# Moving most stores to DRAM from SyncE's queue to GpSimd's queue

## The chip, the cores and the metric

The kernel runs on one core of one Trainium2 chip. The core has five engines with an instruction stream each: TensorE (PE, with its weight loads as PEld), VectorE (DVE), ScalarE (ACT), GpSimd (POOL) and SyncE (SP). An engine works through its stream in order. A transfer between DRAM and on-chip memory (a DMA) is issued by an instruction of one of these streams, and is then carried out by the core's 16 DMA engines. An issue that needs data waits in its stream until the data are there, and what stands behind it in that stream waits too. The metric is the device time of one execution, in microseconds (us).

## The reference, cut to what matters

One layer of a decoder step in fp32, for 1024 tokens of a prompt and 8 samples of 4 tokens (1056 columns in all). Two branches read the same normed input, their results are merged by gates, and a gated ConvFFN follows:

```python
h = rmsnorm(x, norm_mix_g)
z = h @ w_in                                   # 1024 -> 6432 columns
u = zc[..., :D_CONV] * sigmoid(zc[..., D_CONV:])
c, new_conv = causal_dwconv(conv_buf, u, conv_dw_w, conv_dw_b)   # 31 taps
ya = silu(layernorm(c, conv_ln_g, conv_ln_b)) @ w_conv_out
...
# RWKV-7, per token and head of 64:
S = S * w_t + (S a_t) b_t^T + v_t k_t^T ;  y = S r_t
...
yb = ((groupnorm(y) + bonus) * gout) @ w_rw_out
m = gates[..., :D] * ya + gates[..., D:] * yb
x = x + m @ w_mix_out
up = rmsnorm(x, norm_ffn_g) @ w_up             # 1024 -> 6144
f = gelu(conv3(up)[..., :D_FF]) * conv3(up)[..., D_FF:]
x = x + f @ w_down
y = rmsnorm(x, norm_final_g)
```

It also returns the new states: the last 30 convolution inputs, the last projected row, the matrix state S, and the last two up-projected rows.

## The kernel before

**Matmuls.** An fp32 product is split in three products of a faster format: each weight tile (128 x 1024) is loaded raw (L47, `wraw<-w_in`), copied by ScalarE to a high part (L48, `whi`), and VectorE takes the rest as a low part (L49, `wlo`). All matmuls pass through one helper (L54), so rows are told apart by tile: `mm` is a projection of 128 x 352 columns (a block is a third of the 1056 columns), the others (`w`, `c`, `y`) are the small products of the recurrence. There is one buffer for the raw tile before the tail, and two for each part.

**Stages.** `build` runs these after each other.
- Load and norm of the input (0 to some 27 us).
- `mixer_a`: projections of the convolution branch (L324, its 31 taps on VectorE at L359), of the low-rank factors (L553), of the first r, k and v tiles (L457), and the low-rank outputs (L583). Intermediate results that don't fit on chip are stored to DRAM and read back later (`d_cv`, `d_k`, `d_r`, `d_v`, `d_cum`, `d_alr`, `d_gout`).
- `mixer_b` (some 300 to 1380 us): the recurrence. 16 chains, n = 0 to 15, one for each pair of a group of four heads (J) and a quarter of the prompt (q). For each n there is a prep (L892), a stage (L999), a combine (L1065), the chain itself (L1093, it needs the state that chain n-1 left, but for q = 0, where it starts from zeros that GpSimd writes at L1113 and L1115) and a group norm (L1163). The samples' recurrence goes beside it. The remaining projections (r, k, v, gates, convolution output) are the fillers: `drive` (L708) puts them between the steps of the recurrence, by a clock that counts TensorE columns.
- The tail (some 1380 us to the end): merge, output projection and the ConvFFN.

**The turn.** A stage builds triangular 32 x 32 blocks LQ on TensorE and VectorE, stores them (`dL<-LQ`, L1026), loads them back broadcast over the lanes (`L<-dL`, L1028, 512 KB), solves them in 31 steps of two instructions on VectorE (L1034 and L1036, tiles `tm` and `X`), stores the result (`dX<-X`, L1038), and loads it back into LQ (`LQ<-dX`, L1042). Only then can the combine of this n begin. GpSimd clears one block of LQ in each quarter of a stage (L1015) and a tile P in each prep (L910).

**Queues.** In the kernel before, SyncE issues every transfer but eight: loads of weights, stores of intermediate results, the turns, and the outputs. The eight are loads of small parameters at the start, which GpSimd issues (L168). The order of each engine's stream is settled when the program is built: the framework's scheduler takes the instructions by its own estimate of when each can run. A transfer also takes one of eight completion lanes of its kind (SyncE's kind or GpSimd's kind), and waits for the transfer that had this lane before it.

Of the kernel before, what the change touches and what calls it, by code (L numbers as in the profile page):

```python
# [31 lines left out]
class Net:  # L32
# [317 lines left out]
    def conv_taps(self, cv, i):  # L350
        nc = self.nc
        cp, hs, us = cv
        while i not in us:
            yield 1
        c, u, v = us[i]
        cc = slice(i * 128, (i + 1) * 128)
        nc.scalar.activation(out=c[:, 0:TP], in_=u[:, 0:TP], func=AF.Identity, scale=self.col("conv_w", i), bias=self.col("conv_b", i))
        for t in range(1, CW):
            nc.vector.scalar_tensor_tensor(out=c[:, 0:TP], in0=u[:, t:t + TP], scalar=self.col("conv_w", t * 4 + i), in1=c[:, 0:TP],  # L359
                                           op0=ALU.mult, op1=ALU.add)  # L360
            yield

        pr = self.T4("cpr")[:, 0:8 * 4 * CW].rearrange("p (b t w) -> p b t w", b=8, w=CW)
        wt = self.par["conv_w"].rearrange("p (o w i) -> p o w i", o=1, i=4)[:, :, :, i].to_broadcast([128, 8, CW])
        for t in range(4):
            nc.gpsimd.tensor_tensor(out=pr[:, :, t], in0=v[:, :, t:t + CW], in1=wt, op=ALU.mult)
        nc.vector.tensor_reduce(out=c[:, TP:T].rearrange("p (b t) -> p b t", t=4), in_=pr, axis=AX.X, op=ALU.add)
        nc.scalar.activation(out=c[:, TP:T], in_=c[:, TP:T], func=AF.Identity, bias=self.col("conv_b", i))
        nc.sync.dma_start(out=self.d_cv[:, i], in_=c[:, :T])

        ps = self.pw_tile()
        nc.tensor.transpose(ps[:30, 0:128], u[:, TP:TP + 30], self.ident)
        for hf in range(2):
            b = cp.tile([128, 120], F32, tag="cc", name="cc")
            nc.gpsimd.tensor_copy(out=b.rearrange("p (b t) -> p b t", t=30), in_=v[:, hf * 4:hf * 4 + 4, 4:34])
            nc.tensor.transpose(ps[:120, 128 * hf + 128:128 * hf + 256], b, self.ident)
        st = cp.tile([120, 384], F32, tag="cst", name="cst")
        nc.scalar.activation(out=st[:30, 0:128], in_=ps[:30, 0:128], func=AF.Copy)
        nc.scalar.activation(out=st[:, 128:384], in_=ps[:120, 128:384], func=AF.Copy)
        nc.sync.dma_start(out=self.o["p_conv"][0, 0][:, cc], in_=st[:30, 0:128])  # L380
        so = self.o["s_conv"][0].rearrange("b i c -> (b i) c")
        for hf in range(2):
            nc.sync.dma_start(out=so[hf * 120:(hf + 1) * 120, cc], in_=st[:, 128 * hf + 128:128 * hf + 256])

    NLN, LNW = 8, 132

    def ln_block(self, b):

        nc = self.nc
        W = self.LNW  # L390
        s = slice(b * W, (b + 1) * W)
        up = lambda t: t.rearrange("p (o t) -> p o t", o=1).to_broadcast([128, 4, W])
        C, Q = self.T2([128, 4, W], "lnC"), self.T2([128, 4, W], "lnQ")

        def fold(t):

            nc.vector.tensor_tensor(out=Q[:, 0:2], in0=t[:, 0:2], in1=t[:, 2:4], op=ALU.add)
            nc.vector.tensor_tensor(out=Q[:, 0], in0=Q[:, 0], in1=Q[:, 1], op=ALU.add)
        nc.sync.dma_start(out=C, in_=self.d_cv[:, :, s])
        fold(C)  # L400
        yield self.W_LN
        ps = self.pw_tile()
        self.mm(ps[:, 0:W], self.o512, Q[:, 0], True, True)
        nc.vector.tensor_tensor(out=C, in0=C, in1=up(ps[:, 0:W]), op=ALU.subtract)
        nc.scalar.activation(out=Q, in_=C, func=AF.Square)
        fold(Q)
        yield self.W_LN
        ps = self.pw_tile()
        self.mm(ps[:, 256:256 + W], self.o512, Q[:, 0], True, True)
        rs = self.rsqrt((Q[:, 0], Q[:, 1], Q[:, 2]), ps[:, 256:256 + W], 1.0, 1e-5)  # L410
        nc.vector.tensor_tensor(out=C, in0=C, in1=up(rs), op=ALU.mult)
        for i in range(4):
            nc.scalar.activation(out=C[:, i], in_=C[:, i], func=AF.Identity, scale=self.col("cln_g", i), bias=self.col("cln_b", i))
        nc.scalar.activation(out=Q, in_=C, func=AF.Tanh, scale=0.5)
        nc.vector.scalar_tensor_tensor(out=C, in0=Q, scalar=1.0, in1=C, op0=ALU.add, op1=ALU.mult)
        nc.sync.dma_start(out=self.d_cs[:, :, s], in_=C)

    def conv_in(self):

# [12 lines left out]
    def conv_out(self, i):  # L432

        nc, a = self.nc, self.a
        job = lambda i: self.wjob(a["w_conv_out"][0][:, i * 128:(i + 1) * 128], 4)
        w = job(0) if i == 0 else self.cw
        ga = self.cvp.tile([128, T], F32, tag="ga", name="ga", bufs=2)
        nc.sync.dma_start(out=ga, in_=self.d_ga[i])
        if i < ND - 1:
            self.cw = job(i + 1)  # L440
        yield from self.project_g(w, self.cs, 4, lambda b, s, ps: nc.vector.scalar_tensor_tensor(
            out=ga[:, s], in0=ga[:, s], scalar=1.0, in1=ps, op0=ALU.add, op1=ALU.mult))
        nc.sync.dma_start(out=self.d_ma[i], in_=ga)

    def gate(self, i, x):

# [10 lines left out]
    def rkv_tile(self, j, n):  # L457

        nc = self.nc
        jj = (8, 0, 16)[n] + j  # L460
        t = self.T4("krv"[n])
        c0 = ZR + jj * 128
        yield from self.shifted(self.wjob(self.a["w_in"][0][:, c0:c0 + 128]), jj, t)
        nc.sync.dma_start(out=self.d_rkv[n][j // 2][:, j % 2], in_=t)
        self.done.add(("rkv", j, n))

    def shift_state(self):
# [115 lines left out]
    def lora_out(self, j):  # L583
# [27 lines left out]
        cum = self.T4("lc")[:, :T]  # L611
        nc.vector.tensor_tensor_scan(out=cum, data0=rst, data1=sg, initial=0.0, op0=ALU.mult, op1=ALU.add)
        for t, dst in ((cum, self.d_cum), (al, self.d_alr), (go, self.d_gout)):
            nc.sync.dma_start(out=dst[j // 2][:, j % 2], in_=t)


    def wkv_consts(self):
# [216 lines left out]
    def s_shift(self):  # L834

        nc = self.nc
        yield from self.wait(*[("rkv", j, x) for j in range(ND) for x in range(3)])
        for g in range(7):
            yield from self.take(1)
            ps = self.pw_tile()  # L840
            n = 0
            for j in range(4 * g, min(4 * g + 4, NSH)):
                w = min(128, 3360 - j * 128)
                self.tr(ps[:9, n:n + w], self.shcol[:w, j], self.ident[:w, :w])
                n += w
            st = self.T2([9, 512], "sh")
            nc.scalar.activation(out=st[:, :n], in_=ps[:9, :n], func=AF.Copy)
            nc.sync.dma_start(out=self.o["p_shift"][0][:, g * 512:g * 512 + n], in_=st[0:1, :n])
            nc.sync.dma_start(out=self.o["s_shift"][0][:, g * 512:g * 512 + n], in_=st[1:9, :n])
            self.t2_left += 1  # L850
            yield 5000

# [39 lines left out]
    def prep(self, n):  # L892
# [79 lines left out]
        for u in ([slice(0, 1), slice(1, 2)] if smp else [slice(0, 2)]):  # L972
# [1 line left out]
            pv = ps[:, :(u.stop - u.start) * W].rearrange("p (u t) -> p u t", t=W)  # L974
            self.mm(pv, self.bones, t1[:, u], True, True)
            nc.vector.tensor_tensor(out=bv[:, u], in0=pv, in1=v[:, u], op=ALU.mult)
        nc.sync.dma_start(out=self.d_bv[J][:, :, 256 * q:256 * q + 256], in_=bv[:, :, 0:256])

        if smp:
            nc.gpsimd.tensor_copy(out=self.sbv[:, 2 * J % 4:2 * J % 4 + 2], in_=bv[:, :, 256:288])  # L980
# [182 lines left out]
    def group_norm(self, n):  # L1163
# [3 lines left out]
        if q == 3:  # L1167
            yield 800
            ps = self.pw_tile()
            for u in range(2):  # L1170
                self.tr(ps[:64, 128 * u:128 * u + 128], Sf[:, 64 * u:64 * u + 64], self.ident)
            so = self.T2([64, 256], "so")
            nc.scalar.activation(out=so, in_=ps[:64, :256], func=AF.Copy)
            nc.sync.dma_start(out=self.o["p_wkv"][0, 0, 4 * J:4 * J + 4].rearrange("h v k -> v h k"),
                              in_=so.rearrange("p (h k) -> p h k", h=4))
        s = slice(256 * q, 256 * q + 256)
        ld = []
# [22 lines left out]
            self.y_split(slice(2 * J, 2 * J + 2), s, y1)  # L1200
            self.done.add(("y", n))
        else:
            nc.sync.dma_start(out=self.d_y[J][:, :, s], in_=y1)

    def free(self):

# [22 lines left out]
    def samples_in(self, j):  # L1229
# [16 lines left out]
        Sb = self.T2([128, 8, 64], "Sb")  # L1246
        AX_ = self.T2([128, 8, 64], "AXs")
        nc.scalar.activation(out=Sb, in_=ps.rearrange("p (b t) -> p b t", t=64), func=AF.Copy)
        nc.sync.dma_start(out=self.d_S[j], in_=Sb.rearrange("p b t -> p (b t)"))
        ar = ARs.rearrange("p (o q) t -> p o q t", o=1).to_broadcast([128, 8, 2, 32])  # L1250
        mb = self.mb.rearrange("p b (o t) -> p b o t", o=1).to_broadcast([128, 8, 2, 32])
        nc.vector.tensor_tensor(out=AX_.rearrange("p b (q t) -> p b q t", q=2), in0=ar, in1=mb, op=ALU.mult)
# [13 lines left out]
        nc.scalar.activation(out=UV[96:128], in_=ps[0:32, 64:128], func=AF.Copy)  # L1266
        sB = self.T2([64, 128], "sB")
        nc.scalar.activation(out=sB, in_=ps[0:64, 128:256], func=AF.Copy)
        nc.sync.dma_start(out=self.d_BT[j], in_=sB)
        yield 2000  # L1270

        G = self.pw_tile()
# [8 lines left out]
    def samples_steps(self, j0):  # L1281
# [32 lines left out]
        nc.vector.tensor_tensor(out=y1, in0=y1, in1=go, op=ALU.mult)  # L1314
        for n in range(4):
            j = j0 + n
            nc.sync.dma_start(out=self.d_y[j // 2][:, j % 2, TP:T], in_=y1[:, n])

    def samples_state(self, j):

# [17 lines left out]
        for g in range(2):  # L1338
# [4 lines left out]
                self.tr(ps[:64, b * 128:(b + 1) * 128], Sn[:, 4 * g + b], self.ident)  # L1343
            nc.scalar.activation(out=so, in_=ps[:64].rearrange("p (b t) -> p b t", t=128), func=AF.Copy)
            for x in range(2):
                nc.sync.dma_start(out=self.o["s_wkv"][0, 4 * g:4 * g + 4, 2 * j + x].rearrange("b v k -> v b k"),
                                  in_=so[:, :, 64 * x:64 * x + 64])


# [142 lines left out]
    def ffn_up(self, g, fp, cp, uH, uL, rs):  # L1492
# [10 lines left out]
        for n in range(G):  # L1503
            i = g * G + n
            cu = []
            for x in range(2):
# [24 lines left out]
                def rows(n=n, x=x, lr=lr):  # L1531
# [2 lines left out]
                    nc.scalar.activation(out=so[x][:, n * 128:(n + 1) * 128], in_=ps[:18, 0:128], func=AF.Copy)  # L1534
                    if n == G - 1:
                        c = slice(x * DF + g * G * 128, x * DF + (g + 1) * G * 128)
                        nc.sync.dma_start(out=of[0][:, c], in_=so[x][0:16])
                        nc.sync.dma_start(out=of[1][:, c], in_=so[x][16:18])
                self.late.append(rows)

                c = cp.tile([128, T], F32, tag=f"c{x}", name="c", bufs=1)
# [144 lines left out]
```

## Time and profile before

| | before |
|---|---|
| median of the runs | 2556.56 us (2561.31, 2556.56, 2546.82) |
| the profiled execution's own time | 2551.31 us |
| its span, first to last instruction | 2549.6 us |
| mean granted TensorE clock | 0.911 of 2.4 GHz |
| TensorE busy | 2372.1 us, 93% |
| VectorE busy | 1645.4 us, 65% |
| ScalarE busy | 866.1 us, 34% |
| GpSimd busy | 91.9 us, 4% |
| bytes moved by DMA | 230.61 MB, mean 90 GB/s |

The profile is of one execution on the chip. Busy time leaves out the instructions that only issue a transfer or wait for a semaphore, so SyncE has no busy time, and what it issues and waits for is seen in the views of its queue (SPq). TensorE has two clock levels, 1.2 and 2.4 GHz; a granted clock of 0.75 in a stretch is the mean over time at the one and at the other.

### The profile page before, as it was taken

What the parts mean: (1) busy time and instruction counts of PE and PEld (TensorE: products, weight loads), DVE (VectorE), ACT (ScalarE), POOL (GpSimd) and SP (SyncE); (2) the same over time, 40 slices, a digit from 0 to 9 for tenths busy, and PEclk for the clock granted to TensorE, in tenths of its full rate; (3) what the DMA queues carried; (4) which work ended last, traced back from release to release, by engine and by line L of the source; (5) the groups of instructions that cost most, each with busy time, mean ns of one, the idle gap of its engine ahead of it and who ended that gap; (6) DMA issues with size and microseconds to landing.
All of it is one profiled execution on the core that took longest, in us unless ns stands there. A gap on an engine that the chain in (4) does not pass through costs nothing.

```text
span 2549.6 us, 41402 instructions
## 1 busy us (share of the span) xinstructions
PE 2372.1 (93%) x16094; PEld 2147.3 (84%) x16094; DVE 1645.4 (65%) x4174; ACT 866.1 (34%) x1716; POOL 91.9 (4%) x248
## 2 busy tenths in 40 slices
PE   6789989977798789898999999999999999999998
PEld 5778977766676577677778999999999999999998
DVE  5999766777767876786674344465554555545556
ACT  4234332433344344333344222333221322213225
POOL 2301100000000000000000000000000000000000
PEclk9999987966676788689999999999999999999999
DMA  4124443323232343434344664431111111111111
GB/s 123 48 82 161 157 115 83 89 69 100 77 98 63 81 115 85 104 92 117 85 114 137 215 188 137 127 128 44 44 47 48 43 51 44 47 47 40 54 51 69
DMA packets 307637, 230.61 MB, mean 90 GB/s; under 512 B 90492, under 2 KB 287123, under 8 KB 306921
## 3 DMA queue, kind: packets, MB, share of 16 engines
q1 hardware_dynamic: 307185, 227.80, 30.7%
q8 instruction: 127, 2.08, 0.3%
q14 instruction: 69, 0.57, 0.1%
q0 software_dynamic: 256, 0.17, 0.0%
HBM read 157.45 MB, written 70.45 MB: 89 GB/s over the span
## 4 chain that ended last, share of the span: by engine, by line
PE 58%; DVE 4%; DMA 3%; ACT 1%; issue 0%; SPq 0%; DVEq 0%; ACTq 0%
PE mm L54 50%; PE w L54 3%; DMA L<-dL 2%; PE c L54 1%; PE y L54 1%; PE w L61 1%; DMA hL<-d_y 1%; DVE tm L1034 0%; DVE X L1036 0%; PE w L1427 0%; PE w L1512 0%; DMA dX<-X 0%; DVE E L1018 0%; PE mm L1648 0%; PE w L1533 0%
## 5 line engine op out<-in xcount | busy, mean ns | idle before, releaser
L54 PE MATMUL mm<-hH,whi 128*128 128x352 f32 (+1 forms) x2568 | 878.1, 342 | 10.4 <-DVE bcol L496 9.1
L54 PE MATMUL mm<-hH,wlo 128*128 128x352 f32 (+1 forms) x2568 | 855.7, 335 | 20.6 <-DVE wlo L49 20.6
L54 PE MATMUL mm<-hL,whi 128*128 128x352 f32 (+1 forms) x2568 | 857.0, 334 | 0.2 <-DVE hL L248 0.2
L54 PEld LDWEIGHTS mm<-hH,whi 128*128 128x128 f32 (+1 forms) x2568 | 494.5, 193 | 38.3 <-DVE bcol L496 11.2
L54 PEld LDWEIGHTS mm<-hH,wlo 128*128 128x128 f32 (+1 forms) x2568 | 494.9, 193 | 33.0 <-DVE wlo L49 23.1
L54 PEld LDWEIGHTS mm<-hL,whi 128*128 128x128 f32 (+1 forms) x2568 | 495.9, 193 | 10.0 <-issue 1.2
L48 ACT ACTIVATE whi<-wraw 128x1024 fp32r<-128x1024 f32 (+2 forms) x123 | 126.0, 1025 | 403.5 <-PE mm L54 342.9
L1518 DVE TENSOR_TENSOR u<-mm,rs 128x352 f32<-128x352 f32 x144 | 73.5, 511 | 224.6 <-PE mm L54 224.5
L49 DVE TENSOR_TENSOR wlo<-wraw,whi 128x1024 fp32r<-128x1024 f32 (+2 forms) x123 | 146.2, 1189 | 67.8 <-ACT whi L48 67.7
L359 DVE SCALAR_TENSOR_TENSOR sg<-cu,par,sg 128x1024 f32<-128x1024 f32 x120 | 162.6, 1361 | 1.5
L54 PE MATMUL mm<-fH,whi 128*128 128x352 f32 x504 | 163.4, 324 | 0.0
L54 PE MATMUL mm<-fH,wlo 128*128 128x352 f32 x504 | 162.8, 323 | 0.0
L54 PE MATMUL mm<-fL,whi 128*128 128x352 f32 x504 | 162.7, 323 | 0.0
L1573 DVE TENSOR_TENSOR acc<-mm,acc 128x352 f32<-128x352 f32 x168 | 86.9, 522 | 94.0 <-PE mm L54 94.0
L1034 DVE TENSOR_TENSOR tm<-L,X 128x60 f32<-128x60 f32 (+24 forms) x496 | 101.4, 204 | 44.5 <-DMA L<-dL 39.4
L1548 DVE SCALAR_TENSOR_TENSOR c<-u,par,c 128x1024 f32<-128x1024 f32 x96 | 123.0, 1281 | 8.1 <-ACT c L1544 5.2
L54 PE MATMUL w<-E,BK 64*128 64x128 f32 x512 | 95.9, 348 | 17.8 <-DVE BK L990 11.7
L1109 ACT ACTIVATE SP<-UV,PC 64x64 f32<-64x64 f32 x192 | 64.8, 343 | 119.0 <-DVE UV L1149 104.8
L1036 DVE TENSOR_TENSOR X<-X,tm 128x60 f32<-128x60 f32 (+24 forms) x496 | 101.3, 204 | 5.1
L54 PEld LDWEIGHTS w<-E,BK 64*128 64x128 f32 x512 | 78.9, 239 | 29.9 <-DVE BK L990 12.3
L54 PE MATMUL y<-UV,E 128*64 128x64 f32 x512 | 75.8, 270 | 21.6 <-DVE UV L1149 18.4
L54 PEld LDWEIGHTS mm<-fH,whi 128*128 128x128 f32 x504 | 94.8, 188 | 0.5
(379 smaller groups left out, 3547.7 us busy)
## 6 DMA issues: line engine op xcount, KB each, us to landing
wraw<-w_in SPq DMA_DIRECT2D x50, 512.0 KB
wraw<-w_up SPq DMA_DIRECT2D x48, 512.0 KB
wraw<-w_down SPq DMA_DIRECT2D x32, 384.0 KB
L<-dL SPq DMA_DIRECT2D x16, 512.0 KB
d_alr<-la SPq DMA_DIRECT2D x8, 528.0 KB
d_cum<-lc SPq DMA_DIRECT2D x8, 528.0 KB
d_gout<-lg SPq DMA_DIRECT2D x8, 528.0 KB
d_k<-k SPq DMA_DIRECT2D x8, 528.0 KB
```

What stands on the lines that cost most here:

```text
L48: nc.scalar.activation(out=hi[:, :nk, :m], in_=raw[:, :nk, :m], func=AF.Copy)
L49: (lo_eng or nc.vector).tensor_tensor(out=lo[:, :nk, :m], in0=raw[:, :nk, :m], in1=hi[:, :nk, :m].bitcast(F32), op=ALU.subtract)
L54: self.nc.tensor.matmul(out, l, r, start=start, stop=stop)
L61: self.nc.tensor.transpose(out, x, ident)
L359: nc.vector.scalar_tensor_tensor(out=c[:, 0:TP], in0=u[:, t:t + TP], scalar=self.col("conv_w", t * 4 + i), in1=c[:, 0:TP], op0=ALU.mult, o ...
L1034: nc.vector.tensor_tensor(out=tm[:, :a, :m], in0=L[:, s:s + 1, s + 1:32].to_broadcast([128, a, m]), in1=X[:, :a, s:s + 1].to_broadcast([12 ...
L1036: nc.vector.tensor_tensor(out=X[:, :a, s + 1:32], in0=X[:, :a, s + 1:32], in1=tm[:, :a, :m], op=ALU.add)
L1109: nc.scalar.activation(out=at(SP, u, x), in_=src(x)[:, u], func=AF.Copy, scale=PC[hs[x], 4 * u + c:4 * u + c + 1])
L1518: nc.vector.tensor_tensor(out=u[:, 2 + t0:2 + t0 + m], in0=p, in1=rs[:, t0:t0 + m], op=ALU.mult)
L1548: nc.vector.scalar_tensor_tensor(out=c[:, 0:TP], in0=u[:, t:t + TP], scalar=wt, in1=c[:, 0:TP], op0=ALU.mult, op1=ALU.add)
L1573: nc.vector.tensor_tensor(out=acc[i][:, s], in0=ps[:, :BW], in1=acc[i][:, s], op=ALU.add)
```

## The change

At 18 places in the code, `nc.sync.dma_start` becomes `nc.gpsimd.dma_start`; nothing else is edited. Here are the edited lines (unchanged lines around them are left out; a line number is that of the first line of its hunk):

```diff
--- before.py
+++ after.py
@@ -366,7 +366,7 @@
-        nc.sync.dma_start(out=self.d_cv[:, i], in_=c[:, :T])
+        nc.gpsimd.dma_start(out=self.d_cv[:, i], in_=c[:, :T])
@@ -377,10 +377,10 @@
-        nc.sync.dma_start(out=self.o["p_conv"][0, 0][:, cc], in_=st[:30, 0:128])
+        nc.gpsimd.dma_start(out=self.o["p_conv"][0, 0][:, cc], in_=st[:30, 0:128])
-            nc.sync.dma_start(out=so[hf * 120:(hf + 1) * 120, cc], in_=st[:, 128 * hf + 128:128 * hf + 256])
+            nc.gpsimd.dma_start(out=so[hf * 120:(hf + 1) * 120, cc], in_=st[:, 128 * hf + 128:128 * hf + 256])
@@ -413,7 +413,7 @@
-        nc.sync.dma_start(out=self.d_cs[:, :, s], in_=C)
+        nc.gpsimd.dma_start(out=self.d_cs[:, :, s], in_=C)
@@ -440,7 +440,7 @@
-        nc.sync.dma_start(out=self.d_ma[i], in_=ga)
+        nc.gpsimd.dma_start(out=self.d_ma[i], in_=ga)
@@ -461,7 +461,7 @@
-        nc.sync.dma_start(out=self.d_rkv[n][j // 2][:, j % 2], in_=t)
+        nc.gpsimd.dma_start(out=self.d_rkv[n][j // 2][:, j % 2], in_=t)
@@ -611,7 +611,7 @@
-            nc.sync.dma_start(out=dst[j // 2][:, j % 2], in_=t)
+            nc.gpsimd.dma_start(out=dst[j // 2][:, j % 2], in_=t)
@@ -845,8 +845,8 @@
-            nc.sync.dma_start(out=self.o["p_shift"][0][:, g * 512:g * 512 + n], in_=st[0:1, :n])
-            nc.sync.dma_start(out=self.o["s_shift"][0][:, g * 512:g * 512 + n], in_=st[1:9, :n])
+            nc.gpsimd.dma_start(out=self.o["p_shift"][0][:, g * 512:g * 512 + n], in_=st[0:1, :n])
+            nc.gpsimd.dma_start(out=self.o["s_shift"][0][:, g * 512:g * 512 + n], in_=st[1:9, :n])
@@ -974,7 +974,7 @@
-        nc.sync.dma_start(out=self.d_bv[J][:, :, 256 * q:256 * q + 256], in_=bv[:, :, 0:256])
+        nc.gpsimd.dma_start(out=self.d_bv[J][:, :, 256 * q:256 * q + 256], in_=bv[:, :, 0:256])
@@ -1171,7 +1171,7 @@
-            nc.sync.dma_start(out=self.o["p_wkv"][0, 0, 4 * J:4 * J + 4].rearrange("h v k -> v h k"),
+            nc.gpsimd.dma_start(out=self.o["p_wkv"][0, 0, 4 * J:4 * J + 4].rearrange("h v k -> v h k"),
@@ -1200,7 +1200,7 @@
-            nc.sync.dma_start(out=self.d_y[J][:, :, s], in_=y1)
+            nc.gpsimd.dma_start(out=self.d_y[J][:, :, s], in_=y1)
@@ -1246,7 +1246,7 @@
-        nc.sync.dma_start(out=self.d_S[j], in_=Sb.rearrange("p b t -> p (b t)"))
+        nc.gpsimd.dma_start(out=self.d_S[j], in_=Sb.rearrange("p b t -> p (b t)"))
@@ -1266,7 +1266,7 @@
-        nc.sync.dma_start(out=self.d_BT[j], in_=sB)
+        nc.gpsimd.dma_start(out=self.d_BT[j], in_=sB)
@@ -1314,7 +1314,7 @@
-            nc.sync.dma_start(out=self.d_y[j // 2][:, j % 2, TP:T], in_=y1[:, n])
+            nc.gpsimd.dma_start(out=self.d_y[j // 2][:, j % 2, TP:T], in_=y1[:, n])
@@ -1343,7 +1343,7 @@
-                nc.sync.dma_start(out=self.o["s_wkv"][0, 4 * g:4 * g + 4, 2 * j + x].rearrange("b v k -> v b k"),
+                nc.gpsimd.dma_start(out=self.o["s_wkv"][0, 4 * g:4 * g + 4, 2 * j + x].rearrange("b v k -> v b k"),
@@ -1534,8 +1534,8 @@
-                        nc.sync.dma_start(out=of[0][:, c], in_=so[x][0:16])
-                        nc.sync.dma_start(out=of[1][:, c], in_=so[x][16:18])
+                        nc.gpsimd.dma_start(out=of[0][:, c], in_=so[x][0:16])
+                        nc.gpsimd.dma_start(out=of[1][:, c], in_=so[x][16:18])
```

Counted over the loops these are 218 stores. By place in the program: 46 in `mixer_a` (4 of `d_cv`, 12 of the convolution state, 24 of `d_cum`, `d_alr` and `d_gout`, 6 of r, k and v), 100 in `mixer_b` (18 of r, k and v, 8 of `d_cs`, 14 of the shift state, 16 of `d_bv`, 24 of `d_y`, 4 of the matrix state, 16 of the samples' `d_S` and `d_BT`), and 72 from the last part of `mixer_b` on (8 of `d_ma`, 32 of the samples' state, 32 of the ConvFFN's state). These stores stay with SyncE: `dL` and `dX` of the turns, the final output, and also the 16 gate stores at L455 and the 8 stores of `d_x` at L1450, which the diff doesn't touch. All loads stay with SyncE.

The framework's scheduler settles the order again. Three places show what it does.

SyncE, some 700 us into the program (`dX` and `L` are tiles of two different turns, `d_y` is a group norm's result). Before:

```order
L1038 DMA dX_5977<-X 32x8x32 x4
L1028 DMA L<-dL_6374 128x1x1024
L1203 DMA d_y_425<-y_6279 256x1x256
L1042 DMA LQ<-dX_5977 32x8x32 x4
L1249 DMA d_S_2835<-Sb 128x512
L1269 DMA d_BT_2827<-sB 64x128
L900 DMA k<-d_k_480 128x2x256
```

And now, at the same place:

```order
L1028 DMA L<-dL_6374 128x1x1024
L1038 DMA dX_5977<-X 32x8x32 x4
L1042 DMA LQ<-dX_5977 32x8x32 x4
L47 DMA wraw<-w_in 128x8x128
L900 DMA k<-d_k_480 128x2x256
```

The store of `d_y` no longer stands between the stores of `dX` and the loads that bring it back, the samples' stores behind it are gone, and the load of the next `L` has come ahead of the `dX` stores.

GpSimd, where the second group of heads begins (SP is the zero state of a chain, BKs, sbv and ARs are the samples' tiles, P and LQ are cleared for a prep and for a stage). Before:

```order
L915 MEMSET PS 128x16
L1115 MEMSET SP 128x128
L982 TENSOR_TENSOR BKs<-alr,cum 128x2x32
L982 TENSOR_TENSOR BKs<-kn,cum 128x2x32
L980 COPY sbv<-t_5622 128x64
L910 MEMSET P 128x8
L1015 MEMSET LQ 32x4x32 x8
```

And now, at the same place:

```order
L915 MEMSET PS 128x16
L1203 DMA d_y_425<-y_5301 256x1x256
L416 DMA d_cs<-lnC 512x1x132
L1115 MEMSET SP 128x128
L982 TENSOR_TENSOR BKs<-alr,cum 128x2x32
L982 TENSOR_TENSOR BKs<-kn,cum 128x2x32
L464 DMA d_v_489<-v 128x1056
L977 DMA d_bv_2841<-t_5622 256x1x256
L980 COPY sbv<-t_5622 128x64
L910 MEMSET P 128x8
L1015 MEMSET LQ 32x4x32 x4
```

Stores that wait for results of VectorE now stand ahead of the clearing of SP, P and LQ in GpSimd's stream.

VectorE, in the solve of a late turn (X_10487 is the tile that is solved, wlo_11216 the low part of a filler's weights; the number at a row's start is its place in the stream). Before:

```order
2394 L1034 TENSOR_TENSOR tm_10488<-L_10485,X_10487 128x28
2395 L1149 SCALAR_TENSOR_TENSOR UV_9979<-c_10739,PC_9513,SP_10678 64x64
2396 L1036 TENSOR_TENSOR X_10487<-X_10487,tm_10488 128x28
2397 L49 TENSOR_TENSOR wlo_11216<-wraw_11214,whi_11215 128x1024
2398 L1034 TENSOR_TENSOR tm_10488<-L_10485,X_10487 128x2x27
```

And now, where the same `wlo` stands:

```order
2475 L1034 TENSOR_TENSOR tm_10488<-L_10485,X_10487 128x7x5
2476 L1130 COPY R0_11048<-c_11043 128x128
2477 L1036 TENSOR_TENSOR X_10487<-X_10487,tm_10488 128x7x5
2478 L49 TENSOR_TENSOR wlo_11216<-wraw_11214,whi_11215 128x1024
2479 L1034 TENSOR_TENSOR tm_10488<-L_10485,X_10487 128x7x4
```

The same weights are made ready 81 rows later, near the end of the solve instead of near its beginning. On TensorE this shows as fillers that have moved behind the recurrence: up to chain 11 at most 10 filler matmuls (`mm`) more or fewer stand ahead of a chain's first product, and ahead of the first product of chain 15 there are 3205 in the order before and 3067 now, 138 fewer. Until the start of `mixer_b`, TensorE's and VectorE's streams are in the same order.

## Rows read from the trace of the kernel before

**Rows 1.** The page's parts 1 and 2: busy time and share of each engine, and the span in 40 slices of 63.7 us (PE busy and granted TensorE clock, in tenths).

```profile
PE 2372.1 (93%) x16094; PEld 2147.3 (84%) x16094; DVE 1645.4 (65%) x4174; ACT 866.1 (34%) x1716; POOL 91.9 (4%) x248
...
PE   6789989977798789898999999999999999999998
...
PEclk9999987966676788689999999999999999999999
```

**Rows 2.** Busy time of each engine in five stretches of the span, in us, with the number of instructions, the mean granted TensorE clock, the busy share of the DMA engines and GB/s.

```profile
64.00:192.00 128.00, 107.35 (x634) 97.41 (x633) 125.75 (x129) 41.14 (x64) 24.74 (x19) 0.92 0.22 65
192.00:320.00 128.00, 128.00 (x708) 112.64 (x707) 106.28 (x137) 49.82 (x92) 17.59 (x15) 1.00 0.45 158
320.00:1088.00 768.00, 656.38 (x4935) 537.62 (x4934) 558.37 (x2047) 281.02 (x653) 21.27 (x91) 0.75 0.34 90
1088.00:1344.00 256.00, 239.89 (x2015) 195.38 (x2015) 182.80 (x649) 101.82 (x237) 7.16 (x28) 0.93 0.39 101
1344.00:2549.60 1205.60, 1195.86 (x7557) 1167.57 (x7555) 636.62 (x1101) 360.97 (x620) 4.64 (x48) 1.00 0.27 82
```

**Rows 3.** What TensorE waited for between 320 and 1344 us: the waiting group, what released it, us in total, times, the longest.

```profile
PE y L54 <- DVE UV L1149: 18.4, 9, 6.0
PE mm L54 <- DVE wlo L49: 15.2, 7, 6.1
PE w L54 <- DVE t L968: 13.3, 4, 6.7
PE y L54 <- DVE UV L1138: 12.8, 8, 5.8
```

**Rows 4.** The same view of VectorE, 320 to 1344 us.

```profile
DVE tm L1034 <- DMA L<-dL: 39.4, 9, 10.1
```

**Rows 5.** The same view of SyncE's queue (SPq), which issues the transfers, 320 to 1344 us.

```profile
SPq L1203 <- DVE y L1198: 115.3, 12, 18.1
...
SPq L455 <- ACT gt L454: 28.3, 8, 7.8
SPq L464 <- DVE v L486: 27.9, 5, 15.8
...
SPq L416 <- DVE tm L1034: 18.5, 2, 17.3
...
SPq L47 <- DVE wlo L49: 15.1, 2, 7.6
```

**Rows 6.** SyncE's queue in order of time, 702 to 721 us: start, duration, line, operation, out<-in, count.

```profile
702.49 1.80 SPq L1038 DMA_DIRECT2D dX<-X  x4
704.34 0.57 SPq L1028 DMA_DIRECT2D L<-dL  x1
716.10 0.57 SPq L1203 DMA_DIRECT2D d_y<-y  x1
717.16 2.67 SPq L1042 DMA_DIRECT2D LQ<-dX  x4
```

**Rows 7.** The same view of SyncE's queue at 388 to 390 us.

```profile
388.22 0.34 SPq L464 DMA_DIRECT2D d_v<-v  x1
389.73 0.40 SPq L47 DMA_DIRECT2D wraw<-w_in  x1
```

**Rows 8.** The chain that ended last, in order of time: its pieces that are transfers of the turn (start, duration, what).

```profile
856.35 9.63 DMA L<-dL
...
906.31 7.69 DMA dX<-X
...
982.41 10.94 DMA L<-dL
...
1164.85 11.63 DMA L<-dL
...
1236.53 9.90 DMA L<-dL
```

**Rows 9.** GpSimd in order of time at the start: its only eight DMA issues.

```profile
1.37 0.73 POOL L168 DMA_DIRECT2D st<-conv_dw_w  x1 [0.36 <-issue]
...
3.47 0.51 POOL L168 DMA_DIRECT2D st<-conv_ln_b  x1
...
4.50 1.52 POOL L168 DMA_DIRECT2D st<-ffn_dw_w  x3
```

**Rows 10.** What ScalarE and GpSimd waited for between 320 and 1344 us (us in total, times, longest).

```profile
ACT P L911 <- POOL P L910: 7.3, 2, 6.5
...
POOL LQ L1015 <- DVE LQ L1012: 406.0, 55, 54.3
...
POOL P L910 <- PE w L54: 94.8, 4, 39.0
```

**Rows 11.** SyncE's queue in order of time, 64 to 192 us: the first and the last of the 11 issues at L369, L380, L383 and L614.

```profile
101.46 0.37 SPq L380 DMA_DIRECT2D out_p_conv<-cst  x1
...
184.97 0.32 SPq L614 DMA_DIRECT2D d_gout<-lg  x1
```

**Rows 12.** GpSimd's products at L366: their count, ns of the shortest, the median and the longest, first and last start, shapes.

```profile
L366 POOL TENSOR_TENSOR cpr<-us,par x16: 832/1830/1954, 64.6 to 287.2; 128x248 f32<-128x248 f32 x16
```

**Rows 13.** One of GpSimd's groups by line (shapes apart): count, busy us and mean ns of one, idle time before them and what ended it.

```profile
L1015 POOL MEMSET LQ<- 32x128 f32 x64 | 12.7, 198 | 599.2 <-DVE LQ L1012 406.0 <-DVE tm L1034 124.8 <-DVE X L1036 43.5
```

**Rows 14.** TensorE's pace with nothing to wait for: one piece of the chain that ended last (start, duration, what and how many).

```profile
1338.15 11.64 PE mm L54 x72
```

## The prediction

> **What bounds the kernel now.** I read the page first: TensorE is busy for 93% of the span, and the row of slices shows where it isn't: at the start and between slices 5 and 20, where the granted clock falls too [rows 1]. The table of stretches makes this exact [rows 2]. Between 64 and 192 us VectorE is busy for 125.75 of 128 us, so it bounds. From 192 to 320 us, and again from 1344 us to the end, TensorE has next to no gap (1195.86 of 1205.6 us), and a transfer that is issued sooner there can give back no more than the 9.7 us that are idle. What a faster queue can win lies between 320 and 1344 us: 768.00 - 656.38 = 111.6 and 256.00 - 239.89 = 16.1, together 127.7 us of idle TensorE, and there the clock is at 0.75 of its full level, then at 0.93.
>
> Next I read what TensorE waits for in that stretch [rows 3]: results of VectorE, and no transfer among the longest. So SyncE matters only where it is late for VectorE, and the longest row of VectorE's waits is of that kind: 39.4 us in 9 waits for `L`, the broadcast load of the turn [rows 4]. The view of SyncE's own waits is the case for the change [rows 5]: the stores of `d_y` alone hold the queue for 115.3 us in 12 waits, of `d_v` for 27.9 in 5, of `d_cs` for 18.5 in 2. What counts is what stood behind them and who missed it.
>
> **Part by part: what the freed queue gives.** The clearest store in front of a turn is at 716.10 us [rows 6]. The four `dX` stores are issued by 702.49 + 1.80 = 704.29; with the longest landing of `dX` on the chain, 7.69 us [rows 8], they are down by 711.98; the loads back are issued at 717.16, after the store of `d_y`. They come at least 5.2 us late. But in this time TensorE had fillers, and none of its waits in rows 3 is for a transfer or for the combine's input to land. I count this at 0, with 5.2 us as the other end.
>
> The waits for `wlo` cost TensorE 15.2 us [rows 3]. `wlo` comes from a raw load by SyncE, which can have stood behind a store: at 388.22 us `d_v` is issued, and the raw load follows at 389.73 [rows 7]. But SyncE itself waits 15.1 us for `wlo` before it may load [rows 5]: the one raw buffer must be free first. The loop is closed by VectorE, and the queue sits in it only for an issue of 0.40 us. So: 0, and 15.2 us at the other end.
>
> The 39.4 us for `L` are a load that isn't moved. It lands 9.63 to 11.63 us after its issue in the four places where it stands on the chain [rows 8]; the spread of 2.0 us is all that I can lay on stores sharing its queue. At four places that is 8 us at most; I take half, 4 us.
>
> In the tail each store that leaves SyncE saves its issue time, but TensorE has no wait there that it could shorten: 0.
>
> **What GpSimd pays.** Its eight DMA issues of before took from 0.51 to 0.73 us each, three together 1.52 [rows 9]. For 218 stores that is 111 to 159 us more on an engine that is busy for 91.9 us of 2549.6 [rows 1]. It has room; the question is what waits behind them. Clearing LQ (L1015) waits 406.0 us for VectorE and almost nobody waits for it, since the block is needed only after the turn; P (L910) waits 94.8 us for TensorE, and ScalarE in turn waited 7.3 us for P [rows 10]. In mixer_b I count 0 for these, and bound it in the second of the slower rivals.
>
> In the stretch where VectorE bounds, 64 to 192 us, 11 of the stores are issued (6 of the convolution's state, 2 of `d_cv`, 3 of the low-rank outputs) [rows 11]. If each stopped VectorE for its own 0.73 us, that would be 8 us; nothing in the trace shows a DMA issue of GpSimd beside busy VectorE. The nearest row is GpSimd's product at L366, which reads the same memory as VectorE: 832 ns at its shortest, 1830 in the median [rows 12]. Its clearing of LQ, which only writes, takes 198 ns each time [rows 13]. A store's issue has little to read; I take 3 us, with 0 and 11 x 1.83 = 20 us as ends.
>
> The Trainium skill has a sentence on each side. "DMA: Bandwidth & Descriptors", section "Issuing engines are not separate DMA queues", says that issuing from several engines saves only the sequencer's time, since the same 16 engines carry out all of it; by that the sum would be about 0, and the trace agrees in so far as TensorE waits for no transfer. "SBUF — State Buffer", section "SBUF: two separate sides", warns that VectorE, in operations that take both port pairs, keeps GpSimd from writing its descriptors, so that the transfer waits for the end of the operation; by that stores would land later, and it speaks against the change. No run here shows it yet.
>
> **The sum.** Issue times, queue and waits: -4 (for `L`) + 3 (VectorE at the start) + 0 = -1 us against the profiled execution's own 2551.31 us: 2550 us. That execution lies 5.3 us, or 0.2%, under the median of the runs, 2556.56; the forecast is 0.3% under this median. A difference of less than 0.5% (12.8 us) is what a measurement here can't tell from none: the three runs of before differ by 0.57%.
>
> **The rivals.**
>
> Faster. The queue was late more often than I give it. Then the waits for `wlo` go (15.2 us), and the waits for `L` on the chain shorten by 8: 23.2 us, and 2528 us. For it: 115.3 us of SyncE held by one store alone. Against it: the SyncE wait for `wlo` in rows 5, and no row of TensorE that waits for a transfer. The half-speed stretches can add to it: each wait that goes lets the clock rise sooner.
>
> Slower by the new order. The scheduler has taken 138 filler matmuls from ahead of chain 15, since it counts on turns that come sooner. If the turn in the chip is as long as before (9.63 to 11.63 us for `L`, up to 7.69 us for `dX`, rows 8), TensorE reaches the combine of chains 12 to 15 with nothing to do. A filler costs 11.64 / 72 = 0.162 us [rows 14], so 138 x 0.162 = 22.3 us of cover is missing, and the fillers are done later at their full price: 2551.3 + 22.3 = 2574 us. It decides from the point where the solve of chain 12 doesn't end earlier than before. For it: `L` isn't moved, and its landing is most of the turn. Against it: the late weights have let the solve itself run ahead of them.
>
> Slower by GpSimd's stream. The stores' waits (`d_y` 115.3 / 12 = 9.6 us each, the longest 18.1) are now GpSimd's, and the clearing of SP, P and LQ is queued behind them. ScalarE needs P before it can prepare the next stage. If at the four places where a new group of heads begins one store of 9.6 us holds P, and half of this finds no fillers, that is 4 x 9.6 / 2 = 19 us. Contention with VectorE would add 100 stores x 0.73 us x 127.7 / 1024 (the share of time in which TensorE waits) = 9 us. Together 28: 2579 us. For it: ScalarE has already waited 6.5 us for P at a time. Against it: GpSimd waited far longer for others than others for it.
>
> The change doesn't do all it says. 16 gate stores stay with SyncE and hold it for 28.3 us [rows 5], besides the turns. If SyncE's order was what cost time, some of it remains; the time would be that of the forecast, 2550 us.
>
> **How the numbers follow.** No measurable change 0.34, and 0.04 for the part that stays with SyncE; faster 0.34; slower by the order 0.14, slower by GpSimd 0.14. From the forecast's own spread (its terms from -28 to +20) I keep the sides as they are: faster by over 0.5% 0.34, within 0.5% 0.38, slower 0.28. The likeliest case's own range is 2542 to 2566. To leave no more than 2 in 10 out, the range goes down to 2520, the faster case with the late loads of rows 6 added, and up to 2580, where both slower cases end.
>
> **What would show it.** In the profile of the changed kernel, right would be: TensorE's idle time between 320 and 1344 us near 128 us, the same VectorE tiles as its releasers, and VectorE's wait for `L` still at 35 to 40 us. The faster case would show the `wlo` row of TensorE's waits gone, and chain 15 ending well before the rest of the fillers. The slower cases would show TensorE waiting for LQ or the combine's tiles in the last four chains, or ScalarE and TensorE waiting for P, SP or LQ of GpSimd, and issues of GpSimd longer than 0.73 us. VectorE's groups at L359 would be longer in the first 200 us if descriptors and VectorE are in each other's way. The forecast is wrong if VectorE's waits for `L` fall by more than a third, or if GpSimd appears among the releasers of TensorE.

## The result and the profile after

The changed kernel is slower. In 13 runs each its median is 2565.2 us against 2550.66; the ratio is 1.0072, with a 95% interval from 1.0049 to 1.0096. The forecast was no measurable change at 2550 us, within 0.5%; the loss is larger than that. That 2565.2 us lies inside the stated range, and just inside the 2542 to 2566 of the likeliest case, says little for the forecast: both are wider than the loss, and the upper end of the range was set by the two slower rivals. The ratios leave out three executions as slow, all of experiments that change TINV (2578.63, 2582.07 and 5303.98 us). The profiled execution of the changed kernel took 2576.6 us, 25.3 more than that of before, and so lies above its own median; the two profiles are compared for where time goes, the ratio for how much.

The page of the changed kernel, parts 1 to 3:

```profile
PE 2399.1 (93%) x16094; PEld 2170.9 (84%) x16094; DVE 1641.3 (64%) x4174; ACT 867.9 (34%) x1716; POOL 208.6 (8%) x466
...
PEclk9899988967576687768989999999999999999999
...
q1 hardware_dynamic: 270919, 178.83, 24.9%
q0 software_dynamic: 16256, 49.14, 5.5%
```

TensorE has as many instructions as before and is busy for 27 us longer [rows 1]. GpSimd is busy for 208.6 - 91.9 = 116.7 us more, 0.54 us in the mean for each of the 218 stores, and its queue (q0) now moves 49.14 MB. The same stretches as in [rows 2]:

```profile
64.00:192.00 128.00, 106.28 (x627) 96.40 (x625) 125.65 (x128) 40.77 (x63) 27.07 (x31) 0.91 0.22 65
...
320.00:1088.00 768.00, 661.50 (x4941) 543.21 (x4939) 557.04 (x2048) 283.09 (x653) 70.00 (x173) 0.74 0.34 90
1088.00:1344.00 256.00, 240.16 (x1901) 191.66 (x1901) 179.37 (x647) 98.17 (x230) 31.11 (x68) 0.82 0.36 95
```

The last row is the one to learn from. Between 320 and 1344 us TensorE is idle for 106.5 + 15.8 = 122.3 us, less than the 127.7 of before. But from 1088 to 1344 us it runs 1901 matmuls in 240.16 us, where it ran 2015 in 239.89, and the granted clock is 0.82 instead of 0.93. The loss doesn't show as idle time. What TensorE and VectorE wait for there, against [rows 3, 4]:

```profile
PE mm L54 <- DVE wlo L49: 16.6, 9, 6.0
PE w L54 <- DVE t L968: 15.8, 5, 8.7
PE y L54 <- DVE UV L1138: 11.9, 5, 5.8
...
DVE tm L1034 <- DMA L<-dL: 23.3, 5, 8.3
```

Still results of VectorE, and neither a transfer nor GpSimd. VectorE's wait for `L` has fallen from 39.4 to 23.3 us, and the kernel is no faster for it. Next, the ends of the first and the last chain (the last step of each is L1159 on ScalarE) and what is left of the fillers then. Before, ScalarE in order of time, and TensorE's groups from 1380 us to the end (count, busy us, mean ns):

```profile
464.90 0.60 ACT L1159 ACTIVATE Yev<-y 128x512 f32<-128x512 f32 x1 [0.97 <-PE y L54]
...
1378.84 0.60 ACT L1159 ACTIVATE Yev<-y 128x512 f32<-128x512 f32 x1 [5.30 <-PE y L54]
...
L54 PE MATMUL mm<-hH,whi 128*128 128x352 f32 x1455 | 477.8, 328 | 0.1
L54 PE MATMUL mm<-hH,wlo 128*128 128x352 f32 x1455 | 468.6, 322 | 0.0
L54 PE MATMUL mm<-hL,whi 128*128 128x352 f32 x1455 | 467.3, 321 | 0.0
```

And in the changed kernel:

```profile
469.98 0.60 ACT L1159 ACTIVATE Yev<-y 128x512 f32<-128x512 f32 x1 [0.36 <-PE y L54]
...
1379.08 0.60 ACT L1159 ACTIVATE Yev<-y 128x512 f32<-128x512 f32 x1 [4.81 <-PE y L54]
...
L54 PE MATMUL mm<-hH,whi 128*128 128x352 f32 x1497 | 491.3, 328 | 0.5 <-DVE ga L441 0.5
L54 PE MATMUL mm<-hH,wlo 128*128 128x352 f32 x1498 | 482.5, 322 | 0.0
L54 PE MATMUL mm<-hL,whi 128*128 128x352 f32 x1497 | 480.8, 321 | 0.0
```

The last chain ends at 1379.4 us before and at 1379.7 after; from the end of chain 0 to that of chain 15 it is 913.9 us before and 909.1 after. But 4492 of these matmuls remain instead of 4365: 127 more. At the pace of [rows 14], 0.162 us, they take 20.5 us, of the 24.8 us by which the rest has grown (2574.7 - 1379.7 = 1195.0 against 2549.6 - 1379.4 = 1170.2). One new wait there accounts for 3.7 us:

```profile
PE mm L54 <- ACT whi L48: 3.7, 1, 3.7
```

### The profile page after: what moved, and what is told of

Same layout as the page of the kernel before. It is cut to its first block, busy times and chain, and to the rows that moved or that the text cites. A ratio compares the mean times of both kernels' runs of the same rounds, so it can differ in the third digit from the quotient of the medians.

```text
span 2574.7 us, 41582 instructions
## 1 busy us (share of the span) xinstructions
PE 2399.1 (93%) x16094; PEld 2170.9 (84%) x16094; DVE 1641.3 (64%) x4174; ACT 867.9 (34%) x1716; POOL 208.6 (8%) x466
## 3 DMA queue, kind: packets, MB, share of 16 engines
q0 software_dynamic: 16256, 49.14, 5.5%
## 4 chain that ended last, share of the span: by engine, by line
PE 57%; DVE 5%; DMA 3%; issue 1%; ACT 1%; SPq 0%; DVEq 0%; ACTq 0%
PE mm L54 49%; PE w L54 3%; PE c L54 1%; DMA L<-dL 1%; PE w L61 1%; PE y L54 1%; DMA dX<-X 1%; DVE X L1036 1%; DVE tm L1034 1%; DMA hL<-d_y 0%; DVE E L1018 0%; PE w L1427 0%; PE w L1512 0%; DVE UV L1149 0%; DVE LQ L1012 0%
## 5 line engine op out<-in xcount | busy, mean ns | idle before, releaser
L54 PEld LDWEIGHTS mm<-hH,wlo 128*128 128x128 f32 (+1 forms) x2568 | 497.0, 194 | 33.7 <-DVE wlo L49 24.8
L359 DVE SCALAR_TENSOR_TENSOR sg<-cu,par,sg 128x1024 f32<-128x1024 f32 x120 | 164.1, 1373 | 1.5
L54 PE MATMUL w<-E,BK 64*128 64x128 f32 x512 | 103.2, 366 | 18.3 <-DVE BK L990 10.9
L1034 DVE TENSOR_TENSOR tm<-L,X 128x60 f32<-128x60 f32 (+24 forms) x496 | 101.0, 204 | 28.1 <-DMA L<-dL 23.3
L54 PEld LDWEIGHTS w<-E,BK 64*128 64x128 f32 x512 | 84.6, 254 | 31.6 <-DVE BK L990 12.7
L54 PEld LDWEIGHTS mm<-fH,wlo 128*128 128x128 f32 x504 | 95.0, 188 | 0.0
```

Source lines behind the costliest of these rows:

```text
L54: self.nc.tensor.matmul(out, l, r, start=start, stop=stop)
L1034: nc.vector.tensor_tensor(out=tm[:, :a, :m], in0=L[:, s:s + 1, s + 1:32].to_broadcast([128, a, m]), in1=X[:, :a, s:s + 1].to_broadcast([12 ...
```

## The experiments

Two theories. A: the cost is the order; the scheduler takes fillers out of the recurrence and leaves them to the end, wherever the stores are issued. B: the cost is GpSimd as an issuer (its issues, the waits in its stream, contention with VectorE). What makes them separable is that the order of the instructions is known before a run: counted ahead of chain 15's combine (the section on the change counted ahead of the chain's own first product), before has 3206 filler matmuls and the changed kernel 3081, 125 fewer (72 narrow ones of `mixer_a` are left out of both counts), and stores can be picked so that either order comes out with many stores on GpSimd, or few, or none.

**122 stores, the order of before.** Lines 416, 464, 977, 1249, 1269 and 1346 stay with SyncE:

```diff
 # L369, L380, L383, L443, L614, L848, L849, L1174, L1203, L1317, L1537, L1538
-nc.sync.dma_start(...)
+nc.gpsimd.dma_start(...)
```

> 122 of the 218 stores are issued by GpSimd, chosen so that the scheduler leaves as many fillers ahead of chain 15's combine as before (3206; the changed kernel has 3081). Theory A (the cost is the order: 125 fillers at 0.163 us that are left over when the last chain ends): ratio to before 1.000, between 0.997 and 1.003, and chain 15 ends with the fillers of before done. Theory B (the cost is GpSimd as an issuer: its issues, its waits, contention): 122/218 of the 18.4 us that the change costs, 10 us, ratio 1.004, with GpSimd some 65 us busier than before.

> The same kernel as the run with 122 stores on GpSimd and the order of before, to narrow what GpSimd as an issuer costs. Theory A (order): 1.000, between 0.997 and 1.003. Theory B (GpSimd as issuer): 1.004.

Measured: 1.0023 (0.9995 to 1.0052), and again 1.0024 (0.9992 to 1.0056). Most of the loss is gone with more than half of the stores moved. Each interval alone takes in no change, and also theory B's 1.004, so that this kernel by itself doesn't tell the theories apart; the two agree on some 6 us. The stretch from 1088 us in the first of these profiles, as full of matmuls as before:

```profile
1088.00:1344.00 256.00, 240.94 (x2030) 196.00 (x2029) 183.79 (x654) 101.72 (x237) 16.43 (x46) 0.93 0.38 102
```

**8 stores, the order of the changed kernel.** One line is enough to bring the other order out, once with GpSimd and once with ScalarE as issuer:

```diff
-nc.sync.dma_start(out=self.d_cs[:, :, s], in_=C)
+nc.gpsimd.dma_start(out=self.d_cs[:, :, s], in_=C)      # or nc.scalar
```

> Only the 8 stores of d_cs (L416) are issued by GpSimd, all others by SyncE. The scheduler then moves the fillers as in the changed kernel: 3086 ahead of chain 15's combine, 120 fewer than before. Theory A (order): 120 x 0.163 = 20 us slower, ratio 1.005 to 1.009, and after the end of chain 15 some 120 filler matmuls more than before. Theory B (GpSimd as issuer): 8/218 of 18.4 us, 0.7 us, ratio 1.000.

> The 8 stores of d_cs are issued by ScalarE, all others by SyncE; GpSimd issues nothing more than before. The order is the one of the 8-store run (3086 fillers ahead of chain 15's combine). Theory A (order): as slow as with the 8 stores on GpSimd, ratio 1.004 to 1.009. Theory B (GpSimd as issuer): 1.000.

Measured: 1.0063 (1.0031 to 1.0096) with GpSimd, 1.0070 (1.0042 to 1.0098) with ScalarE. Theory B has no room for this: in the second run GpSimd issues nothing that it didn't issue before. The same stretch with 8 stores on GpSimd shows the changed kernel's row, with GpSimd busy for 7.09 us (with ScalarE as issuer the chains ended 12.8 us earlier in the profiled execution, and the stretch has 2016 matmuls at a clock of 0.87):

```profile
1088.00:1344.00 256.00, 238.67 (x1915) 191.56 (x1914) 178.56 (x641) 99.04 (x232) 7.09 (x27) 0.83 0.37 96
```

**No store moved at all.** TINV is the planner's own number for the wait between a stage and its combine (L764 and L997):

```diff
-    TINV = 29750
+    TINV = 29800
```

> The kernel before with TINV 29800 instead of 29750 (21 ns more in the planner's count): no store is moved, but the scheduler leaves 3112 fillers ahead of chain 15's combine, 94 fewer. Theory A: 94 x 0.163 = 15 us slower, ratio 1.003 to 1.008. Theory B: 1.000.

Measured: 1.0058 (1.0030 to 1.0086). The filler groups from 1380 us to the end, 4450 matmuls, 85 more than before:

```profile
L54 PE MATMUL mm<-hH,whi 128*128 128x352 f32 x1483 | 487.0, 328 | 0.0
L54 PE MATMUL mm<-hH,wlo 128*128 128x352 f32 x1484 | 478.0, 322 | 0.0
L54 PE MATMUL mm<-hL,whi 128*128 128x352 f32 x1483 | 476.4, 321 | 0.0
```

So a loss of the size of the change's comes with every store on SyncE. Theory A is shown in this sense; its simple form falls with the next runs.

**More fillers ahead.** TINV 29700 and 28500, each with SyncE's stores and with all 218 on GpSimd:

> The kernel before with TINV 29700: 3296 fillers ahead of chain 15's combine, 90 more. Theory A in its simple form (fillers at 0.163 us): 15 us faster, ratio 0.993 to 0.998; if the chains end later by as much, 1.000, and then the number of fillers alone doesn't tell the time. Theory B: 1.000.

> All 218 stores on GpSimd and TINV 29700: 3288 fillers ahead of chain 15's combine. Theory A: the loss of the change is gone, within 0.3% of the run before with the same TINV. Theory B: 0.7% slower than that run.

> The kernel before with TINV 28500: 3295 fillers ahead of chain 15's combine, all stores on SyncE. Theory A: within 0.3% of the run with the same number and GpSimd's stores, and ratio to before 0.990 to 1.000. Theory B: 0.7% faster than that run.

> All 218 stores on GpSimd, and the wait that the kernel's own planner puts between a stage and its combine (TINV) cut from 29750 to 28500, so that the scheduler leaves 3290 fillers ahead of chain 15's combine (84 more than before, 209 more than the changed kernel). Theory A (order): the loss is gone; ratio to before 0.990 to 1.000, if the chains end no later than 1380 us. Theory B (GpSimd as issuer): still 0.7% slower than the next kernel, which has the same planner's number and SyncE's stores.

Measured: at 29700, 1.0098 (1.0064 to 1.0131) with SyncE and 1.0032 (1.0001 to 1.0063) with GpSimd; at 28500, 1.0041 (1.0013 to 1.0069) with SyncE and 1.0083 (1.0049 to 1.0117) with GpSimd. All four miss what theory A expected: more fillers ahead make nothing faster. Theory B fares no better, which put GpSimd's stores at 0.7% slower both times: at 29700 they are 0.7% faster than SyncE's, and at 28500 0.4% slower, with intervals that overlap. The profiles show where the time goes, when it is read in parts (a chain ends with its last step, as above):

| kernel | fillers ahead | end of chain 0 to end of chain 15, us | chain 15 ends, us | from there to the end, us | ratio |
|---|---|---|---|---|---|
| before | 3206 | 913.9 | 1379.4 | 1170.2 | 1 |
| changed, 218 on GpSimd | 3081 | 909.1 | 1379.7 | 1195.0 | 1.0072 |
| 122 on GpSimd | 3206 | 911.6 | 1382.6 | 1172.7 | 1.0023 |
| the same again | 3206 | 908.3 | 1361.8 | 1172.5 | 1.0024 |
| 8 on GpSimd | 3086 | 908.4 | 1376.2 | 1187.2 | 1.0063 |
| 8 on ScalarE | 3086 | 907.9 | 1363.4 | 1189.8 | 1.0070 |
| TINV 29800 | 3112 | 912.0 | 1376.7 | 1189.9 | 1.0058 |
| TINV 29700 | 3296 | 947.0 | 1401.3 | 1158.6 | 1.0098 |
| TINV 29700, 218 on GpSimd | 3288 | 931.6 | 1402.5 | 1162.8 | 1.0032 |
| TINV 28500 | 3295 | 930.5 | 1385.4 | 1157.0 | 1.0041 |
| TINV 28500, 218 on GpSimd | 3290 | 936.8 | 1412.7 | 1161.6 | 1.0083 |

The last part follows the count of fillers in its direction everywhere: 90 more ahead, and it is 12 to 13 us shorter on SyncE; 94 to 125 fewer, and it is 17 to 25 us longer. The chains answer to one side only. With the fillers of before ahead, or fewer, chains 1 to 15 take 908 to 914 us, whichever queue has the stores; with 82 to 90 more they take 930 to 947, 17 to 33 us longer, for 7 to 13 us that the last part saves. From the end of chain 0 on, the changed kernel is 20.0 us longer than before, and the 122 stores are within 3.3 us of it. So the order of before sits at an edge: the fillers that the change takes out leave the chains no shorter, and further fillers lengthen them.

The time up to the end of chain 0 can't be compared between single profiles. The two of the 122 stores, one kernel, differ by 17.5 us there and by 3.3 us from there to the end of chain 15. Between 384 and 448 us the granted clock was 0.78 in the one and 1.00 in the other. Over all eleven profiles of the table, chain 0 ends at 453 to 456 us where this clock was 0.97 or 1.00, and at 464 to 476 us where it was 0.76 to 0.83.

**Tripling the suspected cost.** The kernel with 122 stores, with two extra issues ahead of each:

```diff
+self.dup(); self.dup()     # nc.gpsimd.dma_start(out=scratch, in_=self.ident[0:1, 0:64])
 nc.gpsimd.dma_start(...)
```

> The run with 122 stores on GpSimd, and ahead of each of them two more DMA issues of GpSimd that store 256 bytes of a constant to scratch: 366 issues on GpSimd, the same order of fillers (3206 ahead of chain 15's combine), next to no more bytes. Nothing of the computation is changed. Theory A: within 0.2% of the run with 122, so 1.000 to 1.004. Theory B: three times the cost of 122 issues, 3 x 0.4% = 1.2%, ratio 1.010 to 1.014.

Measured: 1.0382 (1.0338 to 1.0426), beyond both theories, and for a reason that neither had named. The extra issues depend on nothing, and the scheduler put them at the front, not beside their stores. VectorE's longest wait between 60 and 400 us, what GpSimd waited for, and GpSimd in order of time (lines lie 5 higher here, the products of L366 at L371):

```profile
DVE sg L372 <- POOL cpr L371: 69.0, 2, 55.3
...
POOL dup L56 <- DMA dup<-ident: 44.6, 47, 3.2
...
157.29 0.48 POOL L56 DMA_DIRECT2D dup<-ident  x1 [1.09 <-DMA dup<-ident]
157.79 3.22 POOL L371 TENSOR_TENSOR cpr<-us,par 128x248 f32<-128x248 f32 x4
```

VectorE waited up to 55.3 us for one group of GpSimd's products that stood behind the issues: in this time GpSimd ran 59 of them, 0.48 us each, and they waited 18.2 us more for earlier ones to land. The chains themselves don't suffer: from the end of chain 0 to that of chain 15 it is 1461.0 - 550.7 = 910.3 us here and 1379.4 - 465.5 = 913.9 us before. So the run says nothing on what a store costs in place, but it shows a mechanism of the kind that the second slower rival feared, work that another engine needs held behind issues in GpSimd's stream (there it was P, SP and LQ, here the products of the convolution).

## Why the prediction was wrong

**What bounds** was read rightly: TensorE waits for VectorE, in the changed kernel too, and for no transfer.

**What the freed queue gives** was forecast at 4 us, and no run shows any of it. At the place of [rows 6] SyncE now reads:

```profile
704.26 1.79 SPq L1038 DMA_DIRECT2D dX<-X  x4
709.06 1.78 SPq L1042 DMA_DIRECT2D LQ<-dX  x4
```

The loads back follow the last store by 3.0 us instead of 12.9, which is 9.9 us sooner where I had counted 5.2. The chains as a whole gained nothing by the queue: from chain 0 to chain 15 the changed kernel takes 909.1 us, and the three kernels with as few fillers ahead and next to all stores on SyncE take 907.9 to 912.0. `wlo` costs TensorE 16.6 us instead of 15.2, so the 0 stands. I had named as a sign of error that the wait for `L` falls by more than a third; it fell by 41%, but it is 27.4 us with only 8 stores moved and 28.7 with none moved (TINV 29800), so most of this came with the order rather than with the queue, and what TensorE waits longest for are other results of VectorE.

**What GpSimd pays** was small, as forecast. I had put 3 us for VectorE at the start. From the first instruction at L359 to the first load of the recurrence (L900) it is 253.7 to 253.9 us in the six profiles of the table with SyncE's stores there and 254.8 to 255.5 us in the five with GpSimd's, so 1 to 2 us. They have a visible place. VectorE and GpSimd at 121 us in the changed kernel:

```profile
121.31 0.58 POOL L369 DMA_DIRECT2D d_cv<-sg  x1 [3.62 <-DVE sg L359]
121.49 4.79 DVE L359 SCALAR_TENSOR_TENSOR sg<-cu,par,sg 128x1024 f32<-128x1024 f32 x1
121.97 3.23 POOL L366 TENSOR_TENSOR cpr<-us,par 128x248 f32<-128x248 f32 x4
```

One VectorE instruction that takes 1.28 us in the median takes 4.79, over a GpSimd issue and four GpSimd products that run without a gap. The longest of this group before is 3.34 us; the other kernels of the table repeat both figures, 4.78 to 4.79 with GpSimd's stores there and 3.32 to 3.34 with SyncE's.

What I had not counted is the wait of 3.7 us for `whi` in the tail. It stands in all six profiles in which GpSimd has that part's stores (2.6 to 3.7 us), and is 0.3 us or nothing in the six with SyncE's. In the changed kernel SyncE, which no longer waits for the `d_ma` stores, issues a 512 KB input load (L1402) 0.6 us after a weight load, and 2.8 us after it before; that this load delays the weights is an inference. With the order of before the last part is 2.3 and 2.5 us longer with 122 stores on GpSimd. Together with the 1 to 2 us at the start that makes some 4 us, an estimate from these profiles, which the 1.0023 and its interval allow.

**The step that failed is the sum.** It had terms for the queue, for VectorE and for GpSimd, and none for the 138 fillers that the order shows as moved. They stood only in a rival, with a chance of 0.14. That rival was right in place and size: 22.3 us priced, 20.5 us found in the profile by 127 matmuls, and 1.0058 to 1.0070 measured by orders of this kind with 8 stores or none moved (15 to 18 us). Its condition was that the solve of chain 12 doesn't end earlier. Chain 12 itself did end earlier (1221.0 us against 1233.9), which was my argument against the rival; counted from the end of chain 0 that is 17.9 us, and by chain 15 4.8 us were left, within the spread of the three profiles with the fillers of before (908.3 to 913.9 us). It also named the wrong sign to look for: not TensorE with nothing to do, but the same busy time at a lower clock.

**The rival of GpSimd's stream** (2579 us) didn't happen in the changed kernel: GpSimd is nowhere among the releasers of TensorE, and ScalarE's wait for P is 6.7 us instead of 7.3. The faster rival is out, since the queue was not what TensorE waited for. No run tests what the 24 stores that stayed with SyncE cost.

What stays open: why further fillers ahead lengthen the chains by more than their own time, and how much of the 0.72% exactly is GpSimd's. The runs of the order alone give 1.0058 to 1.0070, the 122 stores alone 1.0023; their intervals are too wide to split the change, and the 4 us above are an estimate from a few profiles. No version tried is faster than the kernel before.

## What to carry to other kernels

An edit that only changes who issues a transfer can also change the program's order wherever a scheduler sets it. Compare the orders first, count what has moved across the last dependent step, and put it into the sum as a term, not into a rival. More fillers ahead are not the cure: here they cost as much on the other side. And control an edit with one that gives the same order without the suspected hardware: here one line, or a planner's number changed by a six-hundredth, cost as much as all 218 stores.

## What the runs showed that was not expected

Idle time hid the loss: with 114 fewer matmuls between 1088 and 1344 us TensorE is busy just as long, at a clock of 0.82 instead of 0.93. The other runs bear this out when the stretch is the last 256 us before the end of chain 15, wherever that lies: 2102 to 2136 matmuls at a clock of 0.96 or 0.97 in the three profiles with the 3206 fillers of before ahead, 1995 to 2022 at 0.85 to 0.89 in the four with fewer. The recurrence's own products `w<-E,BK` take 292 to 305 ns in the mean there in the three, and 327 to 358 ns in the four. And a DMA issue on GpSimd, 0.48 to 0.73 us each in the mean of a group, is cheap until a product that VectorE needs stands behind a row of them: then it cost up to 55.3 us at once.
